# Attention in a hybrid encoder step: four query tiles in one side in place of two, and what TensorE's order of work becomes

## The chip, the cores and the metric

The kernel runs on one core of a Trainium2 chip. The metric is the time of one execution on the device in microseconds (us). The kernel before has a median of 2374.01 us over three runs (2365.21 to 2376.85).

The engines that matter here: TensorE (PE in the profile, its weight loads PEld), VectorE (DVE), ScalarE (ACT), GpSimd (POOL), and SyncE (SP), which issues the DMAs. Each takes its own instructions in the order in which the program has them.

## The reference: what is computed

One inference step of a two-layer encoder: 2048 prompt frames and 32 sample frames of width 1024. Layer 0 is sliding-window attention with a gate, layer 1 a gated DeltaNet. The change touches attention alone:

```
q, k, v, gate = split(h @ w_in)                     # 16 heads of 64, 4 key/value heads
s = einsum('bnqkgd,bnskd->bnkgqs', q, k) * 64 ** -0.5 - slopes * dist
s = where(valid, s, -inf)                           # a 64-frame chunk sees itself and 128 frames before
m = maximum(max(s), sink)
p = exp(s - m);  den = sum(p) + exp(sink - m)
o = einsum('bnkgqs,bnskd->bnqkgd', p / den, v)
y = (o * silu(gate)) @ w_out
```

## The kernel before, in words

The prompt is cut into four slabs of 512 frames (`SLABS`, line 30). The second slab also carries the 32 sample frames, so it is 544 columns wide.

**Blocks.** For each slab `attention_slab` (line 1167) makes 20 input blocks: for each of two groups of key/value heads (gp) a K and a V block (`kv_blocks`, line 989), then four pairs of heads with a q block and a gate block each (`pair`, line 1173). A block is a projection of 128 output features (`project`, line 640): per 512 columns 8 x 3 = 24 matmuls, since every f32 number is split in a high and a low part. Their PSUM banks are called `pj`, two of them. Eight output blocks per slab (`out_blocks`, line 881) multiply the finished heads with `w_out`; they need the slab's attention complete. `pick` (line 550) decides which block is next: output blocks of a slab as soon as its attention is done, else input blocks of the next slab, of which only the first six may come before the output blocks of the slab before.

**Sides.** What isn't a projection runs in generators, "sides", which `step` (line 481) advances between the projection matmuls. The attention of one pair of heads is such a side, `attend` (line 1080). The pair's gate block, when done, starts one side per two query tiles of 128 frames, so two per pair and slab, and in the second slab a third one for the 32 sample frames (lines 1215 to 1220). One side does, in this order:

1. Scores of two tiles by two heads. The two heads lie in partitions 0 to 63 and 64 to 127, so a matmul uses 64 rows of the array (64x128), and head x writes bank x of the two `ta` banks. Three matmuls per tile and head (high by high, high by low, low by high), 12 in all.
2. VectorE adds the bias, takes the row maximum and writes `s` to SBUF, one operation per tile and head (line 1106); then three small ones: maximum with the sink (`mx`), `es`, negation.
3. ScalarE takes the exponential of each with its row sum (line 1119), and of `es`.
4. VectorE: sum, reciprocal, and one scaling per tile and head (line 1126).
5. TensorE transposes the probabilities into the two `tb` banks, eight 128x128 transposes (line 1130), and ScalarE copies each bank to `pt` (line 1144).
6. TensorE multiplies with V into half of the one `tc` bank, 128 rows by 64 columns of the array (128x64), 16 instructions in the trace (line 1151).
7. VectorE multiplies with the gate (`of`, line 1161), ScalarE and GpSimd split the result in high and low part.

A side may begin when the side three before it is through (line 1087). `both` (line 539) takes both banks of a tag, `give` hands them back.

**Banks.** PSUM has eight: `pj` 2, `ms` 1, `ta` 2, `tb` 2, `tc` 1 (line 457).

**The order of the work.** Nothing is issued at once. `Estimate` (line 77) has a price for each operation (lines 119 to 136), and `Order` (line 212) collects all operations of the attention stage with their dependencies and in `flush` (line 313) lays them out by a list schedule: each engine takes, among the operations that are ready by the planner's prices, the one that was asked for first. The result is a fixed order per engine. Operations inside `together` (line 229) form a gang: none of them is ready before all of them are, so they stay in one piece. Before the change the transposes and the V matmuls are gangs, the scores are not. A DMA is tied to a TensorE operation of some time earlier, from the list `past` (line 288), at most to one at 25000 ns of the planner's clock (`START`).

Of the kernel before, what the change touches and what calls it, by code (L numbers as in the profile page):

```python
# [13 lines left out]
AF = mybir.ActivationFunctionType  # L14
ALU = mybir.AluOpType

P = 128
# [5 lines left out]
CH = 64  # L23
WIN = 256
# [52 lines left out]
class Estimate:  # L77
# [19 lines left out]
    def at(self, engine):  # L97
        return self.free.get(engine, 0.0)
# [113 lines left out]
class Order:  # L212
# [46 lines left out]
    def add(self, op, ins, outs):  # L259
        self.rank += 1  # L260
        op.rank = (self.rank - self.lead, self.rank)
        self.ops.append(op)
        waits = {}
        for x, w in [(x, False) for x in ins] + [(x, True) for x in outs]:
            name = x.tensor.name
            if name in self.places:
                self.places[name].ops.append(op)
            elif not name.startswith(SCRATCH):
                continue
            a = self.region(x)  # L270
            bank = x.space == bass.MemoryType.PSUM
            log = []
            for b, bw, o in self.log.get(name, []):
                meet = a[0] < b[1] and b[0] < a[1] and (bank or a[2] < b[3] and b[2] < a[3])
                if o is not op and ((w or bw) and meet or bank and o.engine != op.engine):
                    waits[id(o)] = o
                    if w and a[0] <= b[0] and b[1] <= a[1] and a[2] <= b[2] and b[3] <= a[3]:
                        continue
                log.append((b, bw, o))
            self.log[name] = log + [(a, w, op)]  # L280
        if self.gang and op.engine == "tensor":
            op.gang = self.gang
            self.link(op.gang, op)
        for o in waits.values():
            self.link(o, op)
            if op.gang and o.gang is not op.gang:
                self.link(o, op.gang)
        if op.engine == "tensor":
            self.past.append((self.est.at("tensor"), op))
        elif op.dma:  # L290
            i = bisect.bisect(self.past, min(self.est.at("tensor") - self.EARLY, self.START), key=lambda x: x[0])
            if i:
                self.link(self.past[i - 1][1], op)
# [105 lines left out]
class Kern:  # L399
# [571 lines left out]
    def attention_setup(self, ap):  # L971
        nc = self.nc
        one = lambda shape, tag, dt=F32: self.t(ap, shape, tag, dt, bufs=1)
        self.bias = one([P, HEADS, WIN], "bias")

        def biases():
            for i in range(0, HEADS, 2):
                nc.sync.dma_start(self.bias[:, i : i + 2, :], self.io["bias"][:, i : i + 2, :])
                yield 3000

        self.spawn(biases(), "bias", 12000)

# [4 lines left out]
        self.attended, self.used = set(), [[], []]  # L987

    def kv_blocks(self, slab, si, gp, hT, kv):
        nc = self.nc  # L990
# [89 lines left out]
    def attend(self, me, i, q, sg, gp, vt, og, m, pairs, keyn, tiles, ocol):  # L1080

        nc, ap = self.nc, self.ap
        np_ = len(pairs)
        kh, kl = self.kh[gp], self.kl[gp]
        while me >= 3 and me - 3 not in self.attended:
            yield 100
        yield q
        yield kl  # L1090
        s = self.t(ap, [P, 4, WIN], "s", bufs=3)[:m]
        mx, den, es = [self.t(ap, [P, 2, 2], k, bufs=3)[:m, :np_] for k in ("mx", "den", "es")]
        unit = lambda v, u: v[:, u // 2, u % 2 : u % 2 + 1]

        banks = yield from self.both("ta")
        for a, (qc, kc, lo) in enumerate(pairs):
            for n, (part, k) in enumerate(((0, kh), (0, kl), (1, kh))):
                for x, ps in enumerate(banks):
                    rows = slice(x * CH, (x + 1) * CH)
                    self.mm(  # L1100
                        ps[:m, a * WIN + lo : a * WIN + keyn], q[rows, part, qc : qc + m], k[rows, kc + lo : kc + keyn],
                        n == 0, n == 2)
        yield
        for x, ps in enumerate(banks):
            for a, (qc, kc, lo) in enumerate(pairs):
                nc.vector.tensor_tensor_reduce(
                    out=s[:, 2 * a + x, lo:keyn], in0=ps[:m, a * WIN + lo : a * WIN + keyn],
                    in1=self.bias[:m, 2 * i + x, lo:keyn], scale=1.0, scalar=-3e38, op0=ALU.add, op1=ALU.max,
                    accum_out=unit(mx, 2 * a + x))
            self.give("ta")  # L1110
            yield 0
        yield
        sink = lambda at: self.par[:m, at + 2 * i : at + 2 * i + 2].unsqueeze(1).broadcast_to([m, np_, 2])
        nc.vector.tensor_tensor(out=mx, in0=mx, in1=sink(PC_SK), op=ALU.max)
        nc.vector.tensor_tensor(out=es, in0=sink(PC_SK), in1=mx, op=ALU.subtract)
        nc.vector.tensor_scalar(out=mx, in0=mx, scalar1=-1.0, scalar2=None, op0=ALU.mult)
        for u in range(2 * np_):
            lo = pairs[u // 2][2]
            nc.scalar.activation(s[:, u, lo:keyn], s[:, u, lo:keyn], AF.Exp, bias=unit(mx, u), accum_out=unit(den, u))
        nc.scalar.activation(es, es, AF.Exp)  # L1120
        yield
        nc.vector.tensor_tensor(out=den, in0=den, in1=es, op=ALU.add)
        nc.vector.reciprocal(out=den, in_=den)
        for u in range(2 * np_):
            lo = pairs[u // 2][2]
            nc.vector.tensor_scalar(out=s[:, u, lo:keyn], in0=s[:, u, lo:keyn], scalar1=unit(den, u), scalar2=None, op0=ALU.mult)
        yield
        pts = []
        banks = yield from self.both("tb")
        with self.issue.together():  # L1130
            for a, (ps, tl) in enumerate(zip(banks, tiles)):
                for jj, (blk, vidx, rows) in enumerate(tl):
                    for x in range(2):
                        at = (jj * 2 + x) * P
                        self.tp(ps[:rows, at : at + m], s[:, 2 * a + x, blk * P : blk * P + rows])
        for a, (ps, tl) in enumerate(zip(banks, tiles)):
            pt = self.t(ap, [P, 2, 2, P], "pt", bufs=4)
            if len(tl) == 2 and m == P:
                ev = [(pt.rearrange("p a b t -> p (a b t)"), ps)]
            else:  # L1140
                ev = [(pt[:r, j, :, :m], ps[:r, j * 2 * P : (j + 1) * 2 * P].rearrange("p (x t) -> p x t", x=2)[:, :, :m])
                      for j, (_, _, r) in enumerate(tl)]
            for dst, src in ev:
                nc.scalar.copy(dst, src)
            pts.append((a, pt, tl))
        for _ in banks:
            self.give("tb")
        yield
        yield from og.wait()
        po = yield from self.bank("tc")  # L1150
        with self.issue.together():
            for a, pt, tl in pts:
                for x in range(2):
                    for jj, (blk, vidx, rows) in enumerate(tl):
                        self.mm(
                            po[x * CH : (x + 1) * CH, a * P : a * P + m], vt[:rows, vidx, x * CH : (x + 1) * CH],
                            pt[:rows, jj, x, :m], jj == 0, jj == len(tl) - 1)
        yield
        n = (np_ - 1) * P + m
        of = self.t(ap, [P, 2 * P], "of", bufs=2)  # L1160
        nc.vector.scalar_tensor_tensor(
            out=of[:, :n], in0=po[:, :n], scalar=0.5, in1=sg[:, ocol : ocol + n], op0=ALU.mult, op1=ALU.mult)
        self.split(of[:, :n], og(i, 0)[:, ocol : ocol + n], og(i, 1)[:, ocol : ocol + n], nc.gpsimd)
        self.give("tc")
        self.attended.add(me)

    def attention_slab(self, si, slab, hT, og):
# [5 lines left out]
        def pair(gp, r, kv):  # L1173
# [32 lines left out]
            def attention():  # L1206
# [1046 lines left out]
```

## Time and profile before

| | |
|---|---|
| median of three runs | 2374.01 us (2365.21 to 2376.85) |
| the profiled execution | 2376.4 us, its span 2374.6 us |
| mean granted TensorE clock | 0.978 of full speed |
| attention stage | first scores 36.4 us, last V matmuls 908.7 us |
| DeltaNet stage | after that to the end |

How to read the views: the busy time of an engine is the time in which it has an instruction in work; TensorE's instructions overlap in its pipeline, so the lengths printed for it are latencies, and the start of one to the start of the next is what one costs. Lines of the time-ordered view begin with start and length in us; `x9` means nine like instructions merged; `out<-in` are the program's buffers. In brackets is idle time before the instruction, with what ended it. In the list of waits the columns are total us, times, and the longest. Every operation is issued through one helper, so all have line 185; they are told apart by their buffers: `pj` projections, `ta<-kh,q` and `ta<-kl,q` scores, `tb<-con,s` transposes, `tc<-pt,vt` V products.

### The profile page before, as it was taken

To read this page: it belongs to the slowest core of one execution; us is meant where nothing else is said; L and a number is where in the kernel's file an instruction comes from. 1 tells how busy PE (TensorE), PEld (TensorE's weight loads), DVE (VectorE), ACT (ScalarE), POOL (GpSimd) and SP (SyncE) were. 2 spreads that over 40 slices of the span, in tenths; PEclk is the share of its full clock that TensorE was granted. 3 is DMA by queue.
4 is the path that set the end of the run, shared out by engine and by line. 5 is a ranking of instruction groups with operands and counts; after the bars stand their busy time and mean duration, and the time that the engine had idled before them with its cause. 6 is when DMAs were issued, how large, how long until landed. Compare 5 with 4: busy or idle time off the path is not lost.

```text
span 2374.6 us, 44457 instructions
## 1 busy us (share of the span) xinstructions
PE 2252.8 (95%) x14759; PEld 1843.9 (78%) x14759; DVE 1639.6 (69%) x5024; ACT 1262.2 (53%) x3792; POOL 862.9 (36%) x1044
## 2 busy tenths in 40 slices
PE   8998999999999999999999999989999999999997
PEld 5777788797778777777778788877798767777776
DVE  6765465626553445588887768889786888876876
ACT  5555466636553554455566354564644466445533
POOL 4556555665554334222322121331312222122222
PEclk9998999999999999999999999999999999999998
DMA  7556755585434115544423664333456634466442
GB/s 253 175 187 192 255 188 181 174 279 190 147 105 150 62 63 159 193 149 140 143 89 126 200 227 136 128 115 122 147 172 215 200 118 138 134 215 216 155 142 67
DMA packets 222832, 382.75 MB, mean 161 GB/s; under 512 B 29922, under 2 KB 45194, under 8 KB 222602
## 3 DMA queue, kind: packets, MB, share of 16 engines
q1 hardware_dynamic: 220154, 377.75, 49.4%
q8 instruction: 116, 1.90, 0.3%
q10 hardware_dynamic: 2448, 2.16, 0.3%
q14 instruction: 114, 0.93, 0.1%
HBM read 311.63 MB, written 68.19 MB: 160 GB/s over the span
## 4 chain that ended last, share of the span: by engine, by line
PE 56%; DVE 28%; ACT 7%; issue 4%; DMA 3%; POOL 2%; SPq 0%; DVEq 0%; ACTq 0%; POOLq 0%
PE pj L185 39%; PE tb L185 6%; PE ta L185 5%; PE tc L185 4%; DVE cy L185 4%; DVE s L185 3%; DVE sub L185 3%; DVE tl L185 3%; ACT s L185 2%; DVE ml L185 2%; ACT ta L185 1%; DVE xa L185 1%; DVE r L185 1%; DVE md L185 1%; DVE mx L185 1%
## 5 line engine op out<-in xcount | busy, mean ns | idle before, releaser
L185 PE MATMUL pj<-hk,wh 128*128 128x512 f32 (+1 forms) x8184 | 1770.1, 364 | 26.9 <-DVE xr L185 8.6
L185 PEld LDWEIGHTS pj<-hk,wh 128*128 128x128 f32 x8184 | 1326.6, 191 | 237.9 <-issue 14.1
L185 POOL TENSOR_TENSOR wh<-wr,wh 128x512 fp32r<-128x512 f32 x224 | 295.5, 1321 | 328.2 <-ACT wh L185 283.7
L185 DVE SCALAR_TENSOR_TENSOR cy<-cx,cw,cy 128x512 f32<-128x512 f32 x360 | 230.6, 651 | 44.7 <-ACT cy L185 41.1
L185 ACT CAST wh<-wr 128x512 fp32r<-128x512 f32 x224 | 138.1, 618 | 203.6 <-PE pj L185 157.3
L185 ACT ACTIVATE s<-s,mx 128x256 f32<-128x256 f32 (+1 forms) x272 | 132.0, 487 | 30.1 <-DVE mx L185 29.9
L185 ACT ACTIVATE qs<-tb,egq 64x128 f32<-64x128 f32 x264 | 95.7, 362 | 89.7 <-DVE r L185 76.5
L185 DVE TENSOR_TENSOR sub<-ml,tl 128x60 f32<-128x60 f32 (+24 forms) x527 | 125.8, 239 | 10.2
L185 DVE TENSOR_SCALAR s<-s,den 128x256 f32<-128x256 f32 (+1 forms) x272 | 130.9, 530 | 1.2
L185 ACT ACTIVATE cx<-cy 128x512 f32<-128x512 f32 (+1 forms) x96 | 61.1, 636 | 130.9 <-DVE cy L185 101.5
L185 DVE TENSOR_TENSOR tl<-tl,sub 128x60 f32<-128x60 f32 (+24 forms) x527 | 122.3, 232 | 10.1
L185 DVE CUSTOM_DVE_ANT_0 s<-ta,bias 128x256 f32<-128x256 f32 (+1 forms) x272 | 95.7, 405 | 43.5 <-PE ta L185 42.9
L185 POOL TENSOR_TENSOR pr<-pr,ph 128x512 fp32r<-128x512 f32 x82 | 111.8, 1364 | 34.9 <-ACT ph L185 28.8
L185 POOL COPY cx<-hist 128x3 f32<-128x3 f32 x96 | 25.5, 265 | 263.9 <-DVE kq L185 63.6
L185 DVE TENSOR_TENSOR xr<-pj,xr 128x512 f32<-128x512 f32 (+1 forms) x72 | 41.2, 577 | 112.1 <-PE pj L185 70.1
L185 POOL TENSOR_TENSOR so<-so,mhalf 128x4 f32<-128x4 f32 x33 | 36.8, 1115 | 216.9 <-DVE so L185 189.1
L185 DVE SCALAR_TENSOR_TENSOR r<-tb,nbk,vb 64x128 f32<-64x128 f32 x264 | 91.7, 348 | 29.6 <-PE tb L185 25.1
L185 ACT ACTIVATE qs<-o 128x128 f32<-128x128 f32 x132 | 40.7, 308 | 133.8 <-DVE o L185 128.3
L185 ACT COPY cx<-pj 128x512 f32<-128x512 f32 (+2 forms) x149 | 64.1, 445 | 77.5 <-PE pj L185 62.1
L185 PE MATMUL tb<-st,kq 128*128 128x128 f32 x512 | 94.7, 286 | 6.8 <-DVE st L185 5.9
L185 PEld LDWEIGHTS tb<-st,kq 128*128 128x128 f32 x512 | 82.9, 194 | 21.5 <-DVE st L185 13.0
L185 PE MATMUL tb<-con,s 128*128 128x128 f32 (+2 forms) x528 | 77.7, 280 | 18.9 <-DVE s L185 16.0
(242 smaller groups left out, 3558.0 us busy)
## 6 DMA issues: line engine op xcount, KB each, us to landing
wh<-xswwd SPq DMA_DIRECT2D x528, 256.0 KB
wr<-in_wa SPq DMA_DIRECT2D x160, 256.0 KB
wh<-xswwdo SPq DMA_DIRECT2D x112, 256.0 KB
pr<-in_wd SPq DMA_DIRECT2D x66, 256.0 KB
xswwd<-ph SPq DMA_DIRECT2D x66, 256.0 KB
xswwd<-pr SPq DMA_DIRECT2D x66, 256.0 KB
wr<-in_wao SPq DMA_DIRECT2D x64, 256.0 KB
xa<-in_x SPq DMA_DIRECT2D x48, 256.0 KB
```

The costliest lines, as they stand in the source:

```text
L185: self.order.add(Op(self.name, lambda: call(*args, **kw), cost, op == "dma_start"), ins, outs)
```

## The change

- A side takes all four query tiles of a slab, so there is one side per pair of heads (and the sample side in the second slab). `s` is two of the three buffers, `mx`, `den` and `es` are twice as wide.
- The scores of tiles 0 and 1 go to the two `ta` banks, those of tiles 2 and 3 to the two `tb` banks, all 24 matmuls as one gang.
- The transposes still come as two groups of eight through the `tb` banks, one after the other. When both are asked for, the side is noted in `turned`.
- The V products of all four tiles are one gang of 32 instructions and fill the whole `tc` bank. The product with the gate stays in two halves.
- A side begins when the side two before it is through and the one before it is in `turned`.
- TensorE operations of a gang no longer enter the list `past`.

```diff
-        if op.engine == "tensor":
+        if op.engine == "tensor" and not op.gang:
             self.past.append((self.est.at("tensor"), op))
...
-        while me >= 3 and me - 3 not in self.attended:
+        while me >= 2 and me - 2 not in self.attended or me and me - 1 not in self.turned:
             yield 100
         yield q
         yield kl
-        s = self.t(ap, [P, 4, WIN], "s", bufs=3)[:m]
-        mx, den, es = [self.t(ap, [P, 2, 2], k, bufs=3)[:m, :np_] for k in ("mx", "den", "es")]
+        parts = [range(a, min(a + 2, np_)) for a in range(0, np_, 2)]
+        s = [self.t(ap, [P, 4, WIN], "s", bufs=3)[:m] for _ in parts]
+        at = lambda u: s[u // 4][:, u % 4, pairs[u // 2][2] : keyn]
+        mx, den, es = [self.t(ap, [P, 4, 2], k, bufs=3)[:m, :np_] for k in ("mx", "den", "es")]
...
-        banks = yield from self.both("ta")
-        for a, (qc, kc, lo) in enumerate(pairs):
-            for n, (part, k) in enumerate(((0, kh), (0, kl), (1, kh))):
-                for x, ps in enumerate(banks):
...
+        banks = []
+        for tag, _ in zip(("ta", "tb"), parts):
+            banks.append((yield from self.both(tag)))
+        with self.issue.together():
+            for two, bk in zip(parts, banks):
+                for a in two:
+                    qc, kc, lo = pairs[a]
+                    for n, (part, k) in enumerate(((0, kh), (0, kl), (1, kh))):
+                        for x, ps in enumerate(bk):
...
-        banks = yield from self.both("tb")
-        with self.issue.together():
-            for a, (ps, tl) in enumerate(zip(banks, tiles)):
...
+        for two, sp in zip(parts, s):
+            bk = yield from self.both("tb")
+            if not pts:
+                made = [self.t(ap, [P, 2, 2, P], "pt", bufs=4) for _ in pairs]
+            with self.issue.together():
+                for a, ps in zip(two, bk):
...
+            for _ in bk:
+                self.give("tb")
+            self.turned.add(me)
+            yield
...
-        n = (np_ - 1) * P + m
-        of = self.t(ap, [P, 2 * P], "of", bufs=2)
-        nc.vector.scalar_tensor_tensor(
-            out=of[:, :n], in0=po[:, :n], scalar=0.5, in1=sg[:, ocol : ocol + n], op0=ALU.mult, op1=ALU.mult)
+        for two in parts:
+            c0, n = two[0] * P, (len(two) - 1) * P + m
+            cols = slice(ocol + c0, ocol + c0 + n)
+            of = self.t(ap, [P, 2 * P], "of", bufs=2)
+            nc.vector.scalar_tensor_tensor(
+                out=of[:, :n], in0=po[:, c0 : c0 + n], scalar=0.5, in1=sg[:, cols], op0=ALU.mult, op1=ALU.mult)
...
-                for b in range(0, n // P, 2):
-                    pairs = [(p * P, p * P, 0 if t0 + p else P) for p in (b, b + 1)]
-                    tiles = [[(0, p, P), (1, p + 1, P)][0 if t0 + p else 1 :] for p in (b, b + 1)]
-                    spawn(600 + b * 600, P, pairs, WIN, tiles, b * P)
+                pairs = [(p * P, p * P, 0 if t0 + p else P) for p in range(n // P)]
+                tiles = [[(0, p, P), (1, p + 1, P)][0 if t0 + p else 1 :] for p in range(n // P)]
+                spawn(600, P, pairs, WIN, tiles, 0)
```

More of the change, by code (lines that the diff above doesn't have):

```diff
@@ L986, in attention_setup @@
         self.na = self.nq = 0
-        self.attended, self.used = set(), [[], []]
+        self.attended, self.turned, self.used = set(), set(), [[], []]
     def kv_blocks(self, slab, si, gp, hT, kv):
@@ L1096, in attend @@
-        for a, (qc, kc, lo) in enumerate(pairs):
-            for n, (part, k) in enumerate(((0, kh), (0, kl), (1, kh))):
-                for x, ps in enumerate(banks):
[L1099 to L1102, printed above, removed]
-        yield
[L1104 to L1111, printed above, removed]
+        banks = []
@@ new lines, in attend @@
+        for tag, _ in zip(("ta", "tb"), parts):
[6 more added lines that the diff above has]
+                        for x, ps in enumerate(bk):
+                            rows = slice(x * CH, (x + 1) * CH)
+                            self.mm(
+                                ps[:m, a % 2 * WIN + lo : a % 2 * WIN + keyn], q[rows, part, qc : qc + m],
+                                k[rows, kc + lo : kc + keyn], n == 0, n == 2)
@@ new lines, in attend @@
+        yield
+        for tag, two, bk in zip(("ta", "tb"), parts, banks):
+            for x, ps in enumerate(bk):
+                for a in two:
+                    lo = pairs[a][2]
+                    nc.vector.tensor_tensor_reduce(
+                        out=at(2 * a + x), in0=ps[:m, a % 2 * WIN + lo : a % 2 * WIN + keyn],
+                        in1=self.bias[:m, 2 * i + x, lo:keyn], scale=1.0, scalar=-3e38, op0=ALU.add, op1=ALU.max,
+                        accum_out=unit(mx, 2 * a + x))
+                self.give(tag)
+                yield 0
@@ L1117, in attend @@
         for u in range(2 * np_):
-            lo = pairs[u // 2][2]
-            nc.scalar.activation(s[:, u, lo:keyn], s[:, u, lo:keyn], AF.Exp, bias=unit(mx, u), accum_out=unit(den, u))
+            nc.scalar.activation(at(u), at(u), AF.Exp, bias=unit(mx, u), accum_out=unit(den, u))
         nc.scalar.activation(es, es, AF.Exp)
@@ L1124, in attend @@
         for u in range(2 * np_):
-            lo = pairs[u // 2][2]
-            nc.vector.tensor_scalar(out=s[:, u, lo:keyn], in0=s[:, u, lo:keyn], scalar1=unit(den, u), scalar2=None, op0=ALU.mult)
+            nc.vector.tensor_scalar(out=at(u), in0=at(u), scalar1=unit(den, u), scalar2=None, op0=ALU.mult)
         yield
         pts = []
-        banks = yield from self.both("tb")
-        with self.issue.together():
-            for a, (ps, tl) in enumerate(zip(banks, tiles)):
[L1132 to L1145, printed above, removed]
@@ L1146, in attend @@
-        for _ in banks:
-            self.give("tb")
-        yield
+        for two, sp in zip(parts, s):
[4 more added lines that the diff above has]
+                for a, ps in zip(two, bk):
+                    for jj, (blk, vidx, rows) in enumerate(tiles[a]):
+                        for x in range(2):
+                            col = (jj * 2 + x) * P
+                            self.tp(ps[:rows, col : col + m], sp[:, a % 2 * 2 + x, blk * P : blk * P + rows])
+            for a, ps in zip(two, bk):
+                tl = tiles[a]
+                pt = made[a]
+                if len(tl) == 2 and m == P:
+                    ev = [(pt.rearrange("p a b t -> p (a b t)"), ps)]
+                else:
+                    ev = [(pt[:r, j, :, :m], ps[:r, j * 2 * P : (j + 1) * 2 * P].rearrange("p (x t) -> p x t", x=2)[:, :, :m])
+                          for j, (_, _, r) in enumerate(tl)]
+                for dst, src in ev:
+                    nc.scalar.copy(dst, src)
+                pts.append((a, pt, tl))
+            for _ in bk:
+                self.give("tb")
+            self.turned.add(me)
+            yield
@@ L1158, in attend @@
         yield
-        n = (np_ - 1) * P + m
-        of = self.t(ap, [P, 2 * P], "of", bufs=2)
-        nc.vector.scalar_tensor_tensor(
-            out=of[:, :n], in0=po[:, :n], scalar=0.5, in1=sg[:, ocol : ocol + n], op0=ALU.mult, op1=ALU.mult)
-        self.split(of[:, :n], og(i, 0)[:, ocol : ocol + n], og(i, 1)[:, ocol : ocol + n], nc.gpsimd)
+        for two in parts:
[4 more added lines that the diff above has]
+                out=of[:, :n], in0=po[:, c0 : c0 + n], scalar=0.5, in1=sg[:, cols], op0=ALU.mult, op1=ALU.mult)
+            self.split(of[:, :n], og(i, 0)[:, cols], og(i, 1)[:, cols], nc.gpsimd)
+            yield 0
         self.give("tc")
```

## The prediction

> **What bounds the kernel now.** I read the page first, then the busy time of the engines in the attention stage alone, then what TensorE waited for there.
>
> ```profile
> PE 2252.8 (95%) x14759; PEld 1843.9 (78%) x14759; DVE 1639.6 (69%) x5024; ACT 1262.2 (53%) x3792; POOL 862.9 (36%) x1044
> ```
> ```profile
> 36.00:212.00 176.00, 160.01 (x978) 120.67 (x977) 126.35 (x339) 102.34 (x282) 102.00 (x86) 0.94 0.58 184
> 700.00:910.00 210.00, 209.31 (x1258) 164.49 (x1256) 97.81 (x333) 106.08 (x279) 84.09 (x71) 1.00 0.30 97
> ```
> ```profile
> PE tb L185 <- DVE s L185: 16.0, 20, 2.5
> ...
> PE tc L185 <- ACT pt L185: 6.9, 5, 4.7
> ```
>
> The columns of the second view are the stretch, then busy us of PE, PEld, DVE, ACT, POOL, granted clock, DMA. The change touches only attention, 36 to 910 us. In its last slab (700 to 910) TensorE is busy 209 of 210 us while VectorE and ScalarE are half idle: there a microsecond of TensorE work is a microsecond of time. In the first slab (36 to 212) 16 us of TensorE are idle, VectorE is busy 72% and GpSimd 58%. The third view says what TensorE waits for: the transposes (tb) for the probabilities (s), 16.0 us, and the V products (tc) for the evicted transposes (pt), 6.9 us. So two things can move: the TensorE time of the attention groups, and the 22.9 us of waits in their chain.
>
> Next I read TensorE's order of work for one pair of heads in the last slab, start and length in us:
>
> ```profile
> 839.57 0.39 PE L185 MATMUL ta<-kh,q 64*128 64x256 f32 x2
> 839.79 0.28 PE L185 MATMUL ta<-kl,q 64*128 64x256 f32 x2
> 839.91 0.40 PE L185 MATMUL ta<-kh,q 64*128 64x256 f32 x4
> ...
> 840.47 2.37 PE L185 MATMUL pj<-hk,wh 128*128 128x512 f32 x9
> 842.77 0.39 PE L185 MATMUL ta<-kh,q 64*128 64x256 f32 x2
> ...
> 843.69 5.17 PE L185 MATMUL pj<-hk,wh 128*128 128x512 f32 x21
> 848.70 1.03 PE L185 MATMUL tb<-con,s 128*128 128x128 f32 x8
> 849.49 1.89 PE L185 MATMUL pj<-hk,wh 128*128 128x512 f32 x7
> 851.30 1.15 PE L185 MATMUL tc<-pt,vt 128*64 128x128 f32 x16
> 852.38 0.50 PE L185 MATMUL pj<-hk,wh 128*128 128x512 f32 x1
> 852.72 1.03 PE L185 MATMUL tb<-con,s 128*128 128x128 f32 x8
> 853.51 1.64 PE L185 MATMUL pj<-hk,wh 128*128 128x512 f32 x6
> 855.08 1.14 PE L185 MATMUL tc<-pt,vt 128*64 128x128 f32 x16
> 856.15 1.20 PE L185 MATMUL pj<-hk,wh 128*128 128x512 f32 x4
> 857.27 0.39 PE L185 MATMUL ta<-kh,q 64*128 64x256 f32 x2
> ```
> ```profile
> 914.10 36.70 PE L185 MATMUL pj<-hk,wh 128*128 128x512 f32 x156 [1.42 <-DVE xr L185]
> ```
>
> One pair takes 857.27 - 839.57 = 17.70 us: two sides (two query tiles each), every side a score group (ta), a transpose group (tb) and a V group (tc), with 9+21+7+1+6+4 = 48 projection matmuls (pj) between them. Alone, a pj costs 36.70/156 = 0.235 us, so 48 cost 11.3 and the six groups 6.4, or 3.2 per side. The work in a side is less: scores go two at a time, 839.79 to 839.91 is 0.12 a step, six steps 0.71; eight transposes 849.49 - 848.70 = 0.79, with the start of the next pj 0.87; sixteen V matmuls (1.15 - 0.28)/16 = 0.054 each, 0.87. Sum 2.45. The missing 0.75 us is paid at the edges of the score and V groups, where TensorE goes from 128x128 to 64x128 or 128x64 and back; the transposes stay in 128x128. That is 0.38 us for each score or V group.
>
> **The change part by part.**
>
> *Fewer groups, a gain.*
> ```profile
> L185 DVE SCALAR_TENSOR_TENSOR of<-tc,sg 128x256 f32<-128x256 f32 x64 | 26.9, 420 | 49.7 <-PE tc L185 42.0 <-POOL wh L185 4.3 <-POOL hk L185 2.0
> ```
> 64 full sides become 32, so 32 score groups and 32 V groups go; the matmuls inside stay. 64 x 0.38 = 24 us. Bounds: 0 where the chain and not TensorE sets the pace, 24 where TensorE does; I take 24 and book the chain's part as waits.
>
> *Scores in one piece, a gain.* The 24 score matmuls now become ready together, and the planner can put nothing between. Today it does at times:
> ```profile
> 877.06 0.38 PE L185 MATMUL ta<-kh,q 64*128 64x256 f32 x1
> 877.37 0.50 PE L185 MATMUL pj<-hk,wh 128*128 128x512 f32 x1
> 877.81 0.38 PE L185 MATMUL ta<-kh,q 64*128 64x256 f32 x1
> ```
> Every such cut costs one more pair of edges, 0.38 us. With two cuts a slab it is 3 us, with four 6; I take 3, and 0 as the lower bound.
>
> *Small operations.* The sink maximum, es, negation, sum and reciprocal run once per pair: 32 x 5 fewer on VectorE, 32 fewer on ScalarE. The split of the output into two halves keeps its operations. Neither engine is the bound (VectorE 97.81 of 210 us in the last slab), so I cost this at nothing; its cover is TensorE's own work, and where the chain sets the pace it is a gain of under 1 us a pair, already in the chain below.
>
> *The chain, a loss.* Today two or three half sides overlap: while ScalarE does one's exponentials VectorE does the other's scores. Now a pair is one chain, and the next pair's scores need the tb banks, so they wait until both transposes of this pair are evicted. Its length comes from these rows:
>
> ```profile
> 840.58 0.42 DVE L185 CUSTOM_DVE_ANT_0 s<-ta,bias 128x256 f32<-128x256 f32 x1 [0.41 <-PE ta L185]
> 840.92 0.08 DVE L185 DVE_READ_ACCUMULATOR2_ANT mx<- 128x1 f32 x1
> ...
> 845.92 0.88 DVE L185 TENSOR_SCALAR s<-s,den 128x256 f32<-128x256 f32 x3
> ...
> 849.67 2.17 DVE L185 TENSOR_SCALAR s<-s,den 128x256 f32<-128x256 f32 x4
> ```
> ```profile
> 842.85 0.50 ACT L185 ACTIVATE s<-s,mx 128x256 f32<-128x256 f32 x1
> ...
> 849.63 1.06 ACT L185 COPY pt<-tb 128x512 f32<-128x512 f32 x2
> ```
>
> Counted from the pair's first score: VectorE starts when the ta banks are full, 840.58 - 839.57 = 1.0; eight score evictions at 840.92 - 840.58 = 0.34 make 3.8; to the first exponential 842.85 less the last eviction's end (840.58 + 4 x 0.34 + 0.08 = 842.02) is 0.8, so 4.6; eight exponentials at 0.50 make 8.6; for the sum and the reciprocal ahead of the scalings I put 0.7 (an estimate: two small operations where three fill the 0.8 above, and a hand-over), 9.3; four scalings at 0.29 to 0.54, 10.5 to 11.4, and 0.1 to hand over: the first transposes are ready at **10.6 to 11.5**. Transposes 0.9 and evictions 1.06 come twice: about 4 us more, then the V group. Scores of the next pair can start at 14.6 to 15.5, and ScalarE still has to fit in weight casts and the q and gate evictions. TensorE's demand per pair is 17.70 - 2 x 0.38 = 16.94. So chain and TensorE are nearly level.
>
> What decides is where the planner puts the transposes, because TensorE takes its queue in order: behind a late transpose stand the pj matmuls, for whose banks the q and gate evictions on ScalarE wait, and then the V group. By the planner's prices (lines 119 to 136: 216 ns a pj, 110 a score matmul, which it does not know to run two at a time) the transposes are due about 10.8 us after the first score, of which 24 x 0.11 = 2.6 are scores: it fills the rest with 8.2/0.216 = 38 pj. On the chip these 38 and the scores (12 steps of 0.12 and the edges' 0.38) take 10.7 us against data at 10.6 to 11.5. The wait is 0 to 0.8 per pair; I take 0.5 in the two late slabs. In the two early slabs the scalings are stretched more often. Today's scalings are:
>
> ```profile
> L185 DVE TENSOR_SCALAR s<-s,den 128x256 f32<-128x256 f32 x240 | 116.9, 536 | 1.0
> ```
> That is 0.536 us on average against 0.29 a step in the undisturbed run of three. I take 1.5 there. Sum 16 x 0.5 + 16 x 1.5 = 32 us in place of today's 22.9: a loss of 9, with bounds of -15 (half of them end) and +30 (1.6 a pair everywhere).
>
> The Trainium skill ("SBUF — State Buffer", section "Who interferes with whom") says that a VectorE tensor_scalar in a two-port mode and a GpSimd operation exclude each other, and the loser is fully blocked. The trace agrees in kind (one four takes 2.17, another three 0.88). By that rule alone four scalings in a row are held up once, by 2.17 - 4 x 0.29 = 1.0 us here, in every pair alike: 32 x 1.0 = 32 us of waits, the same term by another split, and the sum stays.
>
> *The sample tile.* In the second slab the 32-row side now goes between two pairs in one line, not beside them. Its chain to the transposes, from the same rows, is 2 x 0.34 + 0.8 + 2 x 0.5 + 0.7 + 2 x 0.3 and an estimated 0.7 of scores and hand-over, about 4.5 us, so a pair and its sample side need 19 to 20 us. TensorE has more to do in that slab too (544 columns in place of 512, plus the sample groups), so most is hidden; I take 3 us in all, with bounds 0 and 8.
>
> *The end of attention.* After the last pair nothing but output blocks is left, and each needs that pair.
> ```profile
> 907.88 1.15 PE L185 MATMUL tc<-pt,vt 128*64 128x128 f32 x16
> ```
> The last two pairs run from 877.06 to 909.03, 32 us. Two chains in line are 2 x 15 to 2 x 16 and a V group of 2: 32 to 34. I take +2, bounds 0 and 6.
>
> *The list of past TensorE operations* that loads are tied to leaves out grouped operations. It only binds loads to the first 25 us of the planner's clock, so at most one early load moves; cost 0, 1 us either way.
>
> **Sum**: -24 - 3 + 9 + 3 + 2 = -13 us. The profiled run took 2376.4 us (span 2374.6), so 2363.4 for it; the median of the three runs is 2374.0, 2.4 lower, and the forecast on that scale is **2361**. The case itself, with waits between 0.6 and 1.5 us a pair (19 to 48 us for 32 pairs) and the other terms as taken, reaches from 2348 to 2377.
>
> **Rivals.**
>
> *The chain takes over, slower.* If the first transposes are late by more than the order allows for, TensorE stands still once per pair. For it: a single stretched scaling is worth 1 us, and there are twice as many scalings in one line. Against it: a pj really takes 0.235 where the planner says 0.216, so TensorE itself comes later than planned. Break-even is (24 + 3 + 22.9 - 5)/32 = 1.4 us a pair. At 2.1 us it is 32 x 2.1 - 22.9 - 27 + 5 = +22, or 2396. Chance 0.20.
>
> *Level, no change.* Chain and TensorE are within 2 us of each other, so the 0.76 saved per pair may only turn into waiting: in the 16 late pairs the pace stays 17.70 and half of the 24 us is lost. Then -12 - 3 + 9 + 5 = -1, or 2373. Chance 0.23.
>
> *Both go well.* If the one-piece groups also end most waits, say 10 us of 22.9 stay: -24 - 3 - 13 + 3 = -37, or 2337. For it: in the last slab the first transposes now start 1.9 us after their data (845.92 + 0.88 to 848.70). Against it: GpSimd is busy 58% of the first slab and stretches the scalings. Chance 0.12.
>
> **How the numbers follow.** The main case has 0.45. A measurement of this kernel tells 0.5% from no change, that is 2362 and 2386. Faster: 0.29 of the main case, all of the last rival, 0.03 of the level one, 0.44. Slower: the first rival and 0.01 of the main case, 0.21. Same: 0.35. The range 2336 to 2392 leaves out about half of the last rival and a part of the first.
>
> **What would show it.** In the changed profile: score groups of 24 and V groups of 32 matmuls without pj between them, about 40 of each; one pair of the last slab in 16.9 to 17.5 us; the waits "tb for s" and "tc for pt" at 25 to 40 us together. It is wrong if a pair still takes 17.7 (level), or if those waits exceed 60 us (chain), and if time moves outside attention, since nothing else was priced.

## The result and the profile after

The changed kernel takes 2405.5 us (median of four runs, 2404.4 to 2409.2) beside 2372.3 us of the kernel before (2365.2 to 2376.9): a ratio of 1.0146, interval 1.0117 to 1.0174. It is slower by 33 us; the forecast was 2361. The profiled execution of after has a span of 2402.7 us, 28.1 us more than before's. In two of the experiments below one run each took 4333 and 7184 us; these two are left out of all medians and ratios.

From the page of after: busy time by engine, then the groups of the scalings and of the transposes (busy us, mean ns, idle before them).

```profile
PE 2253.9 (94%) x14759; PEld 1857.9 (77%) x14759; DVE 1652.3 (69%) x4864; ACT 1258.6 (52%) x3760; POOL 861.6 (36%) x1044
...
L185 DVE TENSOR_SCALAR s<-s,den 128x256 f32<-128x256 f32 (+1 forms) x272 | 175.3, 712 | 1.3
...
L185 PE MATMUL tb<-con,s 128*128 128x128 f32 (+2 forms) x528 | 85.2, 293 | 32.3 <-DVE s L185 22.9
```

The page of before has these two groups as follows:

```profile
L185 DVE TENSOR_SCALAR s<-s,den 128x256 f32<-128x256 f32 (+1 forms) x272 | 130.9, 530 | 1.2
...
L185 PE MATMUL tb<-con,s 128*128 128x128 f32 (+2 forms) x528 | 77.7, 280 | 18.9 <-DVE s L185 16.0
```

VectorE has 160 operations fewer and is busy 13 us longer: the same 272 scalings take 712 ns on average, not 530. From the list of what TensorE waited for, after (us, times, longest):

```profile
PE tb L185 <- DVE s L185: 22.9, 28, 2.1
PE pj L185 <- ACT hk L185: 16.7, 8, 4.2
...
PE tb L185 <- ACT pt L185: 8.2, 6, 3.3
```

The busy time by stretch, after, with the second slab and the end added to those shown of before (columns as there):

```profile
36.00:212.00 176.00, 155.49 (x996) 125.09 (x995) 120.63 (x301) 100.64 (x274) 98.97 (x82) 0.93 0.54 173
212.00:500.00 288.00, 262.98 (x1995) 233.95 (x1994) 152.32 (x424) 152.66 (x419) 156.66 (x138) 0.96 0.57 188
...
700.00:910.00 210.00, 206.85 (x1249) 163.68 (x1247) 100.22 (x282) 105.03 (x272) 88.05 (x78) 1.00 0.30 96
910.00:940.00 30.00, 21.55 (x152) 16.06 (x151) 22.13 (x58) 17.57 (x42) 7.67 (x8) 0.89 0.24 71
```

And the second slab of before:

```profile
212.00:500.00 288.00, 275.26 (x2119) 243.97 (x2120) 151.58 (x472) 160.10 (x442) 170.10 (x147) 0.99 0.63 209
```

In 212 to 500 TensorE has 12 us more idle time and a granted clock of 0.96, not 0.99. Two accounts of the whole stage, worked out from the traces, say where the 28 us are. The first cuts it at marks in the work: the first q eviction of each slab, the last q eviction, the first addition of the last slab's output to `xr` (in us; the last three columns are experiments told below).

| stretch | before | after | e5 before, other scaling | e4 after, other scaling | e7 e4, last pairs split |
|---|---|---|---|---|---|
| slab 0 | 239.8 | 234.1 | 229.3 | 218.3 | 217.5 |
| slab 1 (with the samples) | 260.5 | 278.6 | 259.2 | 260.4 | 258.3 |
| slab 2 | 219.0 | 221.0 | 217.0 | 213.2 | 212.6 |
| slab 3 to its last q | 137.7 | 135.1 | 138.1 | 132.0 | 128.0 |
| end of attention | 24.2 | 36.1 | 25.5 | 35.5 | 28.2 |
| DeltaNet to its last operation | 1457.6 | 1461.9 | 1458.1 | 1460.1 | 1455.7 |

So 18 us were lost in the sample slab and 12 at the end; DeltaNet's 4 are no more than it varies among these versions (1455.5 to 1462.9 over all profiled runs).

The second account takes TensorE from 36 us to the first addition of the last slab's output: its idle time, what the halved clock costs (half of its busy time in stretches granted 0.5), and the rest, which is work at full clock.

| | stage | work | idle | lost to the halved clock | halved stretches |
|---|---|---|---|---|---|
| before | 877.3 | 827.8 | 39.0 | 10.6 | 3 |
| after | 901.1 | 809.2 | 65.6 | 26.3 | 14 |

The change did take 18.6 us of work off TensorE. Idle time gave back 26.6 and the clock 15.7. Each row is one profiled execution, and the single columns vary: e11 below, as long as before, has 36.7 idle and 16.8 lost to the clock.

**What a stretched pair looks like.** TensorE in a pair of slab 1, after (start, length; in brackets the idle time before):

```profile
307.11 8.28 PE L185 MATMUL pj<-hk,wh 128*128 128x272 f32 x64
...
316.56 0.33 PE L185 MATMUL tb<-con,s 128*128 128x128 f32 x1
317.83 0.55 PE L185 MATMUL tb<-con,s 128*128 128x128 f32 x3 [0.95 <-DVE s L185]
319.11 0.33 PE L185 MATMUL tb<-con,s 128*128 128x128 f32 x1 [0.73 <-DVE s L185]
320.37 0.90 PE L185 MATMUL tb<-con,s 128*128 128x128 f32 x3 [0.94 <-DVE s L185]
320.93 2.39 PE L185 MATMUL pj<-hk,wh 128*128 128x272 f32 x9
```

The time-ordered views of VectorE, of GpSimd and of ScalarE around the same moments:

```profile
316.15 5.22 DVE L185 TENSOR_SCALAR s<-s,den 128x256 f32<-128x256 f32 x8
```
```profile
316.32 2.58 POOL L185 TENSOR_TENSOR wh<-wr,wh 128x512 fp32r<-128x512 f32 x2 [5.23 <-ACT wh L185]
318.86 1.31 POOL L185 TENSOR_TENSOR pr<-pr,ph 128x512 fp32r<-128x512 f32 x1
```
```profile
311.35 0.51 ACT L185 ACTIVATE s<-s,mx 128x256 f32<-128x256 f32 x1
...
315.09 0.49 ACT L185 ACTIVATE s<-s,mx 128x256 f32<-128x256 f32 x1
...
315.58 0.60 ACT L185 CAST wh<-wr 128x512 fp32r<-128x512 f32 x1
...
316.38 0.61 ACT L185 CAST wh<-wr 128x512 fp32r<-128x512 f32 x1
316.89 0.62 ACT L185 CAST ph<-pr 128x512 fp32r<-128x512 f32 x1
```

Read them from the bottom. ScalarE has done eight exponentials from 311.35 on, with only their row sums and one q eviction between them; the casts of the next weights come right behind the last. GpSimd subtracts what each cast made, so after 5.23 us of idleness it has three operations in a row, at just the time when VectorE has its eight scalings. The transposes start at 316.56, 317.83, 319.11, 320.37: 1.27 apart, one GpSimd operation (2.58/2). Between two operations of GpSimd VectorE gets one scaling through: taken one by one in the trace, three of the eight take 1.35 to 1.36 us, each ending 0.15 us after one of GpSimd's three operations, and the other five 0.34 to 0.35. It is so in the whole run: each of the 101 scalings of after that take over 0.7 us overlaps a GpSimd operation, on average for 96% of its time (in before all 51, for 94%). TensorE stands at the transposes three times, and from 320.2 to 323.6 the granted clock is 0.5: nine short pj take 323.12 - 320.93 = 2.19 us, 0.24 each where 64 before took (315.31 - 307.11)/64 = 0.13. The next pair has the same gaps and the same halved stretch at 344.1. The pair takes 24.5 us here (scores at 305.48 and 329.94), and 20.5 in before (307.10 and 327.56).

### The profile page after: what moved, and what is told of

It is laid out like the page before. It is cut to its first block, busy times and chain, and to the rows that moved or that the text cites. A ratio compares the mean times of both kernels' runs of the same rounds, so it can differ in the third digit from the quotient of the medians.

```text
span 2402.7 us, 44177 instructions
## 1 busy us (share of the span) xinstructions
PE 2253.9 (94%) x14759; PEld 1857.9 (77%) x14759; DVE 1652.3 (69%) x4864; ACT 1258.6 (52%) x3760; POOL 861.6 (36%) x1044
## 4 chain that ended last, share of the span: by engine, by line
PE 54%; DVE 28%; ACT 8%; issue 4%; POOL 2%; DMA 2%; SPq 0%; DVEq 0%; ACTq 0%; POOLq 0%
PE pj L185 39%; PE tb L185 7%; DVE s L185 5%; PE ta L185 5%; PE tc L185 4%; DVE cy L185 4%; DVE sub L185 3%; DVE tl L185 3%; ACT s L185 2%; ACT ta L185 1%; DVE ml L185 1%; DVE r L185 1%; DVE xa L185 1%; DVE md L185 1%; DVE st L185 1%
## 5 line engine op out<-in xcount | busy, mean ns | idle before, releaser
L185 PEld LDWEIGHTS pj<-hk,wh 128*128 128x128 f32 x8184 | 1337.6, 192 | 251.9 <-ACT hk L185 18.6
L185 DVE TENSOR_SCALAR s<-s,den 128x256 f32<-128x256 f32 (+1 forms) x272 | 175.3, 712 | 1.3
L185 PE MATMUL tb<-con,s 128*128 128x128 f32 (+2 forms) x528 | 85.2, 293 | 32.3 <-DVE s L185 22.9
L185 PEld LDWEIGHTS tb<-con,s 128*128 128x128 f32 (+2 forms) x528 | 65.2, 150 | 53.9 <-DVE s L185 31.5
L185 ACT COPY pt<-tb 128x512 f32<-128x512 f32 (+2 forms) x144 | 71.2, 530 | 64.0 <-PE tb L185 63.5
```

Source lines behind the costliest of these rows:

```text
L185: self.order.add(Op(self.name, lambda: call(*args, **kw), cost, op == "dma_start"), ins, outs)
```

## The experiments

Two theories stood at the start. **Clash**: eight scalings in a row meet a backlog of GpSimd's, each is blocked in its turn, TensorE stands and loses its clock. **Line**: the scalings are not it; the pairs now stand in one line through the `ta` and `tb` banks, in the sample slab with a third side among them, and at the end nothing covers them. Where GpSimd's backlog comes from was asked later, with e9. Ratios are to the kernel before on the same chip, with their intervals. A difference to after in us compares medians of different batches of runs, between which before's own median ran from 2372.3 to 2376.4; where it matters, what the two ratios give (0.001 is 2.4 us) stands beside it. "Long" scalings are those over 0.7 us (worked out from the traces: 51 in before, 101 in after).

**e1: the next pair waits for both transposes.** The code was misread for the prediction, and the description of the change above has it wrong too: `self.turned.add(me)` stands inside the loop over the two halves, so the next pair's scores may go between this pair's two transposes. Here they may not.

```diff
-            self.turned.add(me)
             yield
+        self.turned.add(me)
```

> A pair is noted in turned only after its second transposes, so the next pair's scores can no longer take the tb banks between its two transpose groups. Theory 'line' (the scores of the next pair push the second transposes and the V group back, and at the end of attention nothing fills that): the 12 us lost at the end of attention shrink to 3 or less, the rest stays, about 2396. Theory 'clash' (the scalings on VectorE meet GpSimd's subtractions, TensorE waits for them): no change, 2400 to 2410. If the early scores were a help, filling TensorE's order, it gets slower, over 2412.

Measured: 2438.3, ratio 1.0257 (1.0241 to 1.0273), 33 us slower than after (26 by the ratios). TensorE's wait for the scaled probabilities doubles:

```profile
PE tb L185 <- DVE s L185: 48.7, 56, 6.8
```

Idle 87.2, lost to the clock 37.2, work 809.6, long scalings 105. The early scores are no part of the loss: they cover it, and without them it would have been nearly twice as large.

**e2: the sample slab with sides of two tiles, the rest as after.** A side begins by the rule of before where neither it nor the two sides ahead of it have four tiles; that part of the edit is not shown, here or in e3, e7 and e8.

```diff
...
-                spawn(600, P, pairs, WIN, tiles, 0)
+                if smp:
+                    for b in range(0, n // P, 2):
+                        spawn(600 + b * 600, P, pairs[b : b + 2], WIN, tiles[b : b + 2], b * P)
+                else:
+                    spawn(600, P, pairs, WIN, tiles, 0)
```

> Only the second slab, the one with the sample frames, goes back to sides of two tiles; the other three slabs keep four. Between the first q eviction of that slab and its last output the changed kernel lost 20 us against before. Theory 'sample line' (the sample side stands between two pairs and makes the chain longer than TensorE's work): those 20 us come back, about 2385. Theory 'clash' predicts the same for this slab, since two-tile sides spread the scalings, but then the long scalings (over 0.7 us) of this slab fall from 28 to about 11. If the loss is general, only a quarter of the 33 us comes back: 2397.

Measured: 2387.6, ratio 1.0048 (1.0033 to 1.0064). That is 18 us faster than after (23 by the ratios). Slab 1 is 262.6 us long, 16 less than in after, with 17 long scalings in place of 32. So some 16 us are lost in that slab; whether by its clashes or its line, this doesn't tell.

**e3: the last two pairs of the last slab with sides of two tiles.** The same edit with the condition `si == len(SLABS) - 1 and i >= 6`.

> Only the last two pairs of the last slab go back to sides of two tiles. Theory 'end' (with whole pairs the two last chains stand one behind the other and the output blocks run out of work): the stretch from the last q eviction to the first output block loses 12 us less, about 2393. If the end merely shows what was late before it, nothing changes: 2400 to 2408.

Measured: 2395.7, ratio 1.0077 (1.0055 to 1.0099), 10 us faster than after (16 by the ratios); the end takes 28.8 in place of 36.1, slab 3 131.0 in place of 135.1. The end is a loss of its own.

**e4: after, with the scaling in a form that also sums its output.** The sum is written to a buffer that nobody reads.

```diff
+        one = self.t(ap, [P, 4, 2], "one", bufs=3)[:m, :np_]
...
-            nc.vector.tensor_scalar(out=at(u), in0=at(u), scalar1=unit(den, u), scalar2=None, op0=ALU.mult)
+            nc.vector.tensor_scalar(
+                out=at(u), in0=at(u), scalar1=unit(den, u), scalar2=0.0, op0=ALU.mult, op1=ALU.add, accum_out=unit(one, u))
```

> The scaling of the probabilities writes an accumulator as well, which costs VectorE about 0.1 us more per operation (8 a pair) but should keep it from being blocked by GpSimd. Theory 'clash': long scalings fall from 101 to near 0, TensorE's waits for s from 22.9 us to under 10, time 2385 or less. Theory 'line' or 'sample line': scalings get shorter, but the time moves by under 5 us, as the chain's order stays.

Measured: 2351.4, ratio 0.9894 (0.9865 to 0.9923): 54 us faster than after (60 by the ratios), and 25 faster than before. The group on the page, and one run of scalings in slab 1 with GpSimd beside it:

```profile
L185 DVE TENSOR_SCALAR_CACHE_REDUCE s<-s,den 128x256 f32<-128x256 f32 (+1 forms) x272 | 108.4, 461 | 1.3
```
```profile
300.26 0.48 DVE L185 TENSOR_SCALAR_CACHE_REDUCE s<-s,den 128x256 f32<-128x256 f32 x1
300.66 0.08 DVE L185 DVE_READ_ACCUMULATOR s<-s,den 128x1 f32 x1
300.66 0.48 DVE L185 TENSOR_SCALAR_CACHE_REDUCE s<-s,den 128x256 f32<-128x256 f32 x1
```
```profile
300.03 2.53 POOL L185 TENSOR_TENSOR wh<-wr,wh 128x512 fp32r<-128x512 f32 x2 [3.78 <-ACT wh L185]
302.52 1.28 POOL L185 TENSOR_TENSOR pr<-pr,ph 128x512 fp32r<-128x512 f32 x1
```

GpSimd has the same backlog in the same place, and the scalings go on in steps of 0.40 us, none over 0.481 in the whole run. TensorE idle 38.4, lost 11.4, work 805.5. The Trainium skill ("SBUF — State Buffer", section "Who interferes with whom") excepts the form of tensor_scalar that also writes out its accumulator from those that can take the ports shared with GpSimd; the run agrees, with 0 long scalings in place of 101.

**e5: the kernel before with the same scaling.**

> The kernel before, with the accumulating form of the scaling alone. Theory 'clash is the price of the change' (the four-tile chain meets GpSimd twice as often): before has 51 long scalings to the changed kernel's 101, and about 15 us of waits behind them, so it gains 10 to 25 us: 2352 to 2366, less than half of the 54 us that the changed kernel gained. Rival 'the form helps alike': it gains 45 us or more, 2330, and the change is still slower by some 30 us without any clash.

Measured: 2362.8, ratio 0.9944 (0.9929 to 0.9959), 13 us faster than before. So the clash cost 13 us there and 54 to 60 in after, and without it the change gains 2362.8 - 2351.4 = 11 us (12 by the ratios).

**e6: the plan of e4, the instruction of after.** The planner sees the second output of the accumulating form, so e4 has another order of work than after in places (TensorE's is the same in 13944 of 14759). Here it plans that form and the plain one is issued; the three other engines' orders are e4's, TensorE's in 14747 of 14759 places.

```diff
...
+            if op == "tensor_scalar" and "accum_out" in kw:
+                kw = {k: v for k, v in kw.items() if k not in ("accum_out", "op1")} | {"scalar2": None}
```

> The planner is given the accumulating scaling, so the order of all engines is that of the run with the accumulating form, but the plain scaling is issued. Theory 'clash': the long scalings are back (90 to 110) and the time is that of the changed kernel, 2395 to 2415. Rival 'another order': the 54 us came from the slightly different order that the planner laid out, and the time stays at 2351 to 2360.

Measured: 2411.5, ratio 1.0148 (1.0132 to 1.0163). The page's group of scalings:

```profile
L187 DVE TENSOR_SCALAR s<-s,den 128x256 f32<-128x256 f32 (+1 forms) x272 | 176.7, 717 | 1.3
```

Long ones 101, as in after. One form of one instruction is worth 60 us in all but the same order of work. From e4 to e6 TensorE's idle time goes from 38.4 to 72.2 us, what it loses to the clock from 11.4 to 33.1, and its work from 805.5 to 808.9. Of the 33.8 us of idle time 24.2 are its wait for the scaled probabilities, first in e4, then in e6:

```profile
PE tb L185 <- DVE s L185: 4.3, 6, 2.5
```
```profile
PE tb L187 <- DVE s L187: 28.5, 37, 2.6
```

**e7 and e8: e4 with the last two pairs split as in e3; e8 with the sample slab split too.**

> The changed kernel with the accumulating scaling, and sides of two tiles for the last two pairs of the last slab. If clash and end add up, 8 to 12 us less than with the accumulating form alone (2351): 2339 to 2343. If the end was only slow because of the clashes, no change: 2347 to 2356.

> As the run before, and the slab with the sample frames in sides of two tiles as well. Theory 'clash': with short scalings the sample slab loses nothing by the line, so it is within 5 us of the run with the last two pairs alone. Theory 'sample line': the line costs by its length too, 10 us or more come back: 2332 or less.

Measured: e7 2339.2, ratio 0.9847 (0.9831 to 0.9864); e8 2338.6, ratio 0.984 (0.9815 to 0.9866). The split at the end brings 12 us on top of e4. The split of the sample slab brings nothing more that shows (the two intervals allow some 7 us either way) once the clash is gone, so what was lost there were in the main clashes and not the line. e7 beats both kernels, after by 66 us and before by 36.

**e9: after, with the weight casts ahead.** If ScalarE's eight exponentials dam up the casts, casts that may go between them should thin GpSimd's backlog. The casts get the planner's precedence of evictions.

```diff
...
+            self.issue.lead = Order.EVAC
...
+            self.issue.lead = 0
```

> The changed kernel with the plain scaling; only the planner's priority of the weight casts on ScalarE is raised, so that they go between the exponentials and not behind all eight. Theory 'queue' (the casts wait behind eight exponentials in a row, so GpSimd's subtractions that follow them fall into the scalings): GpSimd works during the exponentials again (share over 0.2, now 0.08), long scalings drop from 101 to 50 to 80, time 2375 to 2395. If the clash comes from the scalings being eight in a row, wherever the casts are, the count and the time stay: over 2400.

Measured: 2389.2, ratio 1.0062 (1.004 to 1.0084), 16 us faster than after (20 by the ratios). The scalings on the page:

```profile
L185 DVE TENSOR_SCALAR s<-s,den 128x256 f32<-128x256 f32 (+1 forms) x272 | 134.5, 563 | 1.2
```

Worked out from overlaps: GpSimd is busy during 0.39 of the exponentials' time (0.08 in after, 0.35 in before) and 0.59 of the scalings' (0.74, 0.55); long scalings 64. So the dam is a source of the backlog, and opening it gives back 16 to 20 of the 54 to 60 us; where the rest of the backlog comes from was not tested. The slab with the samples keeps its length, though, 277.8 us, with 23 long scalings; why the gain is in the other slabs (5 us each in slabs 0 and 2) was not settled.

**e10: e4 with the edit of e1.**

> The accumulating scaling, and the next pair's scores wait for both transposes of a pair, as my prediction had read the change. With the plain scaling that cost 33 us. If the cost was a longer chain under clashes, little is left: 2351 to 2360. If the chain of one whole pair at a time is too long by itself, it costs 20 us or more here too: 2371 or more.

Measured: 2363.5, ratio 0.9946 (0.9929 to 0.9963), 12 us slower than e4, between the two expectations. Late scores cost 26 to 33 us with the clash and 12 without. Of these, the account has 6 as idle time and 8 as work; the latter was not explained.

**e11: before with its scores as gangs** (`with self.issue.together()` around them, and the same line of `past` as in the change).

> The kernel before, its scores issued in one piece (12 matmuls) and nothing else. My prediction gave 3 us for fewer cuts, at most 6: 2370 to 2376. If waiting for all four operands of a group costs TensorE order, it is slower: 2378 or more.

Measured: 2378.3, ratio 1.0008 (0.9995 to 1.0022): no change from the two together.

**e12: e7 with the casts of e9.**

> The best so far (accumulating scaling, last two pairs in two-tile sides, 2339) with the casts ahead. Without a clash to avoid the earlier casts only lengthen the exponentials' stretch: no gain, 2337 to 2348. If earlier weights still help, under 2334.

Measured: 2350.6 (three runs), ratio 0.9896 (0.9861 to 0.993), slower than expected. Where nothing clashes, early casts bring nothing and probably cost some 11 us, with intervals that just touch; no trace tells why.

## Why the prediction was wrong

**Edges, -24: right as work.** The rows below are TensorE in the last slab, after:

```profile
788.77 0.39 PE L185 MATMUL ta<-kh,q 64*128 64x256 f32 x2
...
790.39 2.60 PE L185 MATMUL pj<-hk,wh 128*128 128x512 f32 x10
792.83 1.03 PE L185 MATMUL tb<-con,s 128*128 128x128 f32 x8
793.62 6.09 PE L185 MATMUL pj<-hk,wh 128*128 128x512 f32 x25
799.64 2.02 PE L185 MATMUL tc<-pt,vt 128*64 128x128 f32 x32
801.58 2.81 PE L185 MATMUL pj<-hk,wh 128*128 128x512 f32 x11
804.23 1.03 PE L185 MATMUL tb<-con,s 128*128 128x128 f32 x8
805.02 3.51 PE L185 MATMUL pj<-hk,wh 128*128 128x512 f32 x14
808.46 0.39 PE L185 MATMUL ta<-kh,q 64*128 64x256 f32 x2
```

24 scores take 790.39 - 788.77 = 1.62 us, where before had twice 0.90; 32 V products 801.58 - 799.64 = 1.94, twice 1.08 before. That is 0.40 a pair; with the two entrances saved, 0.15 to 0.18 each by the pj ahead of them, 0.7 to 0.8 as priced. In the accounts the work falls by 18.6 from before to after and by 828.8 - 805.5 = 23.3 from e5 to e4. In time: from the first q eviction of the last slab to its last, seven pairs on, after takes 137.7 - 135.1 = 2.6 us less than before, 0.4 a pair, so an estimated 17.3 for one pair, as forecast; e4 takes 138.1 - 132.0 = 6.1 less than e5, 0.9 a pair.

**Cuts of score groups, -3: not found.** e11 has it, with the list `past`, and shows nothing. The V groups of all 32 pairs are whole, and the score groups of 30. A gang isn't always in one piece, as the description above has it: at the end the scores of a pair lie in pieces among projections, from 892.86 to 899.92 us.

**Small operations, nothing:** no sign against it.

**The chain, +9: the step that failed, in size and in picture.** Its picture had the next pair's scores wait for both transposes. In the rows above the scores at 788.77 come before the transposes of 792.83, which belong to the pair before; two pairs overlap, and e1 shows that this is worth 26 to 33 us. That error made the forecast too dark. The other was larger and the other way: it took 0.5 to 1.5 us of waiting a pair, and let a run of four scalings be held up once, by 1.0 us. The page of the Trainium skill that it cites there ("SBUF — State Buffer", section "Who interferes with whom") says that one engine is blocked for the other's whole instruction; that it happens once in a run was the prediction's own step. The rows at 316 us show the blocked engine let through for one operation and blocked again, for as long as GpSimd has a backlog, and the change adds to that backlog by putting eight exponentials in a row (e9, for a part of it). The sum had 9 us for this term; the clash costs 54 to 60 us in after (e4, e6) and 13 in before (e5), so the term should have been 41 to 47; with the 11 us that the change gains without the clash this makes 30 to 36, and 33 were measured. For the clock, which took 15.7 us more than in before, the sum had nothing and gave no reason. (Two of its figures are off, with little in the sum behind them: the bounds by its own words are -11 and +28, not -15 and +30, and a scaling alone takes 0.26 us a step, not a third of 0.88.)

The test named for it didn't ring: the waits "tb for s" and "tc for pt", forecast at 25 to 40, came to 25 (22.9, and 2.0 in place of 6.9), so it looked as if the chain had held. Against before the loss lies in waits under other names and in the clock, which no list of waits shows. The largest of these waits, in the attention stage, first of before, then of after:

```profile
PE pj L185 <- ACT hk L185: 0.9, 2, 0.5
```
```profile
PE pj L185 <- ACT hk L185: 13.2, 5, 4.2
```

Of this at least 4.23 + 1.36 = 5.6 us belong to the end below.

**The sample tile, +3:** the line itself costs nothing that e8 can show against e7. The 18 us of that slab go with the clash (260.4 us in e4, 259.2 in e5).

**The end, +2: 10 to 12.** TensorE there, after:

```profile
900.86 1.35 PE L185 MATMUL tb<-con,s 128*128 128x128 f32 x8
...
918.53 2.02 PE L185 MATMUL tc<-pt,vt 128*64 128x128 f32 x32
924.78 1.22 PE L185 MATMUL pj<-hk,wh 128*128 128x512 f32 x2 [4.23 <-ACT hk L185]
...
931.53 2.02 PE L185 MATMUL tc<-pt,vt 128*64 128x128 f32 x32
934.91 0.73 PE L185 MATMUL pj<-hk,wh 128*128 128x512 f32 x2 [1.36 <-ACT hk L185]
```

The last scores start only at 912.60 and their V group at 931.53; nothing is left to fill the gap, and the clock is 0.5 for 6.8 us from 924.3. The prediction laid two chains end to end and asked only how long they are. Split in two, the chains of e7 overlap: its last V matmuls come in pieces from 862.60 to 870.55 with projections between, and its end is 28.2 us.

**Sum.** With 18.6 for the work that left, no cuts, 26.6 of idle time and 15.7 of lost clock, the stage gets 23.7 us longer; 4 us more lie in DeltaNet. The rival that ended slower (2396) had the right place, TensorE standing at the transposes, and the right suspect; it asked for 2.1 us a pair in place of before's 0.7 (22.9/32), so 1.4 more, and (26.6 + 15.7)/32 = 1.3 more were measured, over a third of it in the clock, which it hadn't counted.

## What to carry to other kernels

When two small groups are merged into a large one, ask of each engine in the chain what queues behind its longer run, and where that backlog then falls; here a run of eight on ScalarE moved a part of GpSimd's work onto VectorE's next run. Add up the bottleneck engine's work, idle time and lost clock separately, since a list of waits shows only part of a loss. And before restructuring look for the same operation in a form that the other engine does not hold up: that one line gained 13 us alone, and the change then 11 more.

## What the runs showed of the hardware

A plain scaling of 128x256 takes 0.26 us a step alone (the last four of the eight at 316 us start 0.26 apart), and about 1.3 behind each operation of a GpSimd backlog. GpSimd is hardly slowed in turn: its subtractions for wh in the stage take 1.30 us with the clash (after, median; mean 1.33) and 1.29 without (e4; 1.31). The form that also sums takes 0.40 a step beside GpSimd's backlog and never over 0.48 us (e4), so it is slower alone and cheaper here (108.4 us for 272, against 175.3).

Three idle times of 0.7 to 0.95 us within 4 us were followed by a stretch of 3.4 us at half clock, in two pairs at the same place; there are 14 such stretches of 3.4 or 6.8 us in after's attention, 5 in e4's and 2 in e7's. That the gaps cause them is read from this order and from their going together; no run tests it alone. The Trainium skill ("TensorE: Matmul & The Clock Gate", section "A second HAM failure mode: psum-queue depth-cycling") tells of short idle times between groups of matmuls that make the clock swing; the rows agree.
